# Where the modulation dots and the projection pieces stand among the steps of a head pair, in the first attention of a two-layer diffusion trunk

## The chip, the cores and the metric

One core of a Trainium2 chip runs the whole program: TensorE (PE, with its weight loads PEld), VectorE (DVE), ScalarE (ACT), GpSimd (POOL) and SyncE (SP), which issues all the DMAs. The metric is device time of one execution in microseconds; before the change the median of 3 runs is 1429.26 us (1427.46 to 1429.32).

## What is computed

Two layers over 1024 latent tokens and 256 context tokens of width 1024 (16 heads of 64). Each layer modulates its input, projects it, mixes, gates, projects out and normalises. Cut to what matters here:

```python
for i in range(DEPTH):                                            # DEPTH = 2
    shift, scale, gate = split(silu(c) @ w_ada[i] + b_ada[i], 3)  # the modulation; also with c_ctx
    u = h * (1 + scale) + shift
    y, yc = mixer_a(u, uc, ...) if i == 0 else mixer_b(u, uc, ...)
    h = layer_norm(ALPHA * h + gate * y, ...)

def mixer_a(u, uc, ...):
    q, k, v, g = split(u @ w_in)               # 16 query heads, 4 key/value heads
    q, k = rope(q), rope(k)                    # latents only
    # 128 queries at a time, against 3 blocks of 128 keys, the 256 context keys and a sink logit
    p = softmax(concat([mask(q @ k.T * scale), q @ k_ctx.T * scale, sink]))
    y = (p @ v * silu(g)) @ w_out
```

## The kernel before, in words

**Precision.** Every fp32 operand is split into a high and a low part, and a product is three matmuls (hi·hi, hi·lo, lo·hi), so TensorE is the busy engine throughout.

**The first attention (mixer a)** goes over 8 head pairs p. A pair has 20 *subs*: ten blocks b of 128 queries (8 of latents, 2 of context) for two heads h. Sub k = 20p + 2b + h does the following. `qkA` (L729): four score matmuls S_A (L739, L740) into a PSUM tile; `sm_first` (L308): DVE reads S_A, adds the mask and takes the row extreme (L320, I call it the *read* of S), POOL copies the sink in (L325), ACT takes the exponential (L327); `sm_second`: DVE reciprocal (L331), POOL scales (L332); `trA` (L753): TensorE transposes the 2, 4 or 5 blocks into another PSUM tile T_A (L339), ACT copies it out as the high part (L343), DVE subtracts for the low part (L345, the *split* of T); `pvA_fn` (L760): TensorE multiplies with the values (L768), and after each second block ACT and DVE combine the halves (L777, L779) and POOL gates (L782).

S_A and T_A share one PSUM tag `big` with **two** buffers (L97). So a T can begin only when the tile that had its buffer before has been let go: an S by its read L320, a T by its split L345; the same holds for an S.

**Steps.** `att_steps` (L786) makes the rows of this work. In the row where sub k's scores are issued, sub k-3 is transposed (AHEAD_A = 3) and one half of a block's value product is done. So in rows 0 to 2 of a pair the *last* three subs of the pair before are transposed, which are context blocks and narrow (two blocks, 256 columns), and the first scores of the new pair are issued. I call this place the *seam*. The rows of pair p are `rowsA[20p : 20p+20]`.

**Projection pieces.** Between the steps stand pieces of the projections for the gate of pair p and the queries of pair p+1: `gprojA(p) + qprojA(p+1)`, 48 pieces of three matmuls pj (L210 to L212), each 512 columns wide, or 256 for the context chunk. `merge` (L287) walks both lists by their costs: a piece is taken whenever the share of piece cost done is not above the share of step cost done. A step costs 545 for the transposes, 545 for the scores, 545 for half a value product; a piece 653 or 326. Evacuating a query chunk is the rope on DVE, POOL and ACT (L499 to L502) and the high and low parts for two heads (L694 on ACT, L695 on DVE, tiles qA).

**Modulation dots.** 48 dots (`dot_half`, L636) build the rest of the first layer's modulation and the second layer's in pairs 0 to 6 (SEG: 7 per pair, 6 in the last), off TensorE. One dot issues a DMA of 256 KB (L650, tile gw, two buffers), a multiply-and-sum on DVE (L652), a multiply on POOL (L653), and, at the next dot's place, a sum on ACT (L634). After the last of them `dots_end` (L658) does twelve small DVE operations (L662 to L667). Before the change they are inserted into the list of a pair's steps at positions 3, 12, 21 and so on, which is in rows 1, 3, 6, 9, 11, 14 and 17 or near them.

**What decides the order.** The program order of `merge` is not yet the order on the engines: the tile framework schedules each instruction by priority and by its own estimates, and `lift` (L130) raises some (the reads by LIFT_A = 80, the splits by 60). Each engine then takes its own list strictly in order. PSUM buffers of a tag are handed out in this scheduling as well, so which tile a T waits for can differ from row to row. Keys: the two heads' pairs 2q and 2q+1 share keys; `k_load(p // 2, 1)` (L713, tile kA) loads the second key tile of the new group when an even pair begins.

Of the kernel before, what the change touches and what calls it, by code (L numbers as in the profile page):

```python
# [38 lines left out]
GATED_LAST = 1 << 20  # L39

SEG = (7, 7, 7, 7, 7, 7, 6, 0)


def f32(ap):
    return ap.bitcast(F32)
# [37 lines left out]
def build(tc, i, out):  # L83
# [203 lines left out]
    def merge(att, fill, lead=0.0):  # L287

        ta = sum(a[0] for a in att) or 1.0
        tf = sum(f[0] for f in fill)  # L290
        ia = jf = 0
        ca = cf = 0.0
        while ia < len(att) or jf < len(fill):
            need = att[ia][2] if ia < len(att) and len(att[ia]) > 2 else 0
            if jf < len(fill) and (ia == len(att) or jf < need or cf - lead <= ca * (tf - lead) / ta):
                cf += fill[jf][0]
                fill[jf][1]()
                jf += 1
            else:
                ca += att[ia][0]  # L300
                att[ia][1]()
                ia += 1
# [333 lines left out]
    def dot_half(h, j):  # L636
        def run():
            dot_sum()
            if j == 0:
                gh.clear()  # L640
                for v in range(2):
                    t = px.tile([P, 512], F32, tag=f"gh{v}", bufs=1, name="gh")
                    dma(t, bass.AP(i["cr"].tensor, v * D + h * 512, [[0, P], [1, 512]]))
                    th = px.tile([P, 512], F32, tag="gw", bufs=2, name="gth")
                    nc.scalar.activation(th, t, AF.Tanh, scale=0.5)
                    nc.vector.scalar_tensor_tensor(t, th, 1.0, t, ALU.add, ALU.mult)
                    gh.append(t)
            acc = dhalf if h else dcol
            t = px.tile([P, 512], F32, tag="gw", bufs=2, name="gw")
            dma(t, i["wadaT"][j, :, h * 512 : (h + 1) * 512])  # L650
            o = ap_.tile([P, 512], F32, tag="ra", bufs=1, name="gj")
            nc.vector.tensor_tensor_reduce(o, t, gh[0], 0.5, 0.0, ALU.mult, ALU.add, accum_out=acc[:, j, 0:1])  # L652
            nc.gpsimd.tensor_tensor(t, t, gh[1], ALU.mult)  # L653
            sums.append((t, acc[:, j, 1:2]))

        return (0.0, run, 0)
# [12 lines left out]
    dots = [dot_half(h, j) for h in range(2) for j in range(24)]  # L669
# [29 lines left out]
    def qprojA(p):  # L699
        return proj_pieces(pos["Aq", p], uA, CHUNKS, rope_evac(q_store(p), ap_, 1))  # L700
# [9 lines left out]
    def k_load(kv, l):  # L710
        k = pq.tile([P, T], F32R, tag="kA", bufs=3, name=f"kA{kv}_{l}")
        for x in range(2):
            dma(f32(k[x * 64 : x * 64 + 64]), kdA[l, kv * 64 : kv * 64 + 64, :])  # L713
        kA[kv, l] = k

    def v_loadA(kv):
        v = pq.tile([P, 10, P], F32R, tag="vA", bufs=2, name=f"vA{kv}")
        dma(f32(v), vdA[:, kv, :].rearrange("(t p) e -> p t e", p=P))
        vA[kv] = v
# [40 lines left out]
    def pvA_fn(p, b, part):  # L760
        if b % 2 == 0 and part == 0:
            pvA[p] = psone(f"pvA{p}_{b}")
        o = pvA[p][:, (b % 2) * 256 : (b % 2) * 256 + 256]
        tl = tilesA(b)
        pt = ptA[p, b]
        for k, t in enumerate(tl):
            x = (pt.lo if part else pt.hi)[:, k].rearrange("p h q -> p (h q)")
            mm(o, vA[p // 2][:, t, :], x, start=k == 0 and not part, stop=part == 1 and k == len(tl) - 1)  # L768
        if not part:
            return  # L770
        del ptA[p, b]
        if b % 2 == 1:
            tmp = px.tile([P, 2, P], F32, tag="otmp", bufs=1, name="otmp")
            pv = pvA[p].rearrange("p (b h q) -> p b h q", b=2, h=2)
            heads = [(h, slice(h * 64, h * 64 + 64)) for h in range(2)]
            for h, hs in heads:
                nc.scalar.copy(tmp[hs], pv[64:128, :, h, :])  # L777
            for h, hs in heads:
                nc.vector.tensor_tensor(tmp[hs], pv[0:64, :, h, :], tmp[hs], ALU.add)  # L779
            tok = slice((b - 1) * P, (b + 1) * P)  # L780
            g = gA[p][:, tok]
            nc.gpsimd.tensor_tensor(g, tmp.rearrange("p b q -> p (b q)"), g, ALU.mult)  # L782
            if p == 7:
                dma(ogd[p][:, tok], g)
            elif b == 9:
                dma(ogd[p], gA[p])  # L786

    def att_steps(subs, qk, st, tr, pv, last_of_unit, costs, need, ahead, rise, split=False):

        seq = []  # L790
        n = len(subs)
        for k in range(-ahead, n + 2 + split):
            row = []

            def t_piece(k=k):
                if k + 1 < n:
                    with lift(rise(k)):
                        sm_second(st[k + 1])
                if k >= 0:
                    tr(k)  # L800

            def s_piece(k=k):
                qk(k + ahead)

            def v_piece(k=k):
                pv(k - 2)

            def v_first(k=k):
                pv(k - 2, 0)

            def v_second(k=k):
                pv(k - 3, 1)

            if -1 <= k < n:
                row.append((costs[0] if k >= 0 else 0.0, t_piece, 0))
            if k + ahead < n:
                row.append((costs[1], s_piece, 0))
            if split and 0 <= k - 2 < n and last_of_unit(k - 2):
                row.append((costs[2] / 2, v_first, 0))
            elif split and k - 3 >= 0 and last_of_unit(k - 3):  # L820
                row.append((costs[2] / 2, v_second, need(k - 3, k + ahead)))
            elif not split and k - 2 >= 0 and last_of_unit(k - 2):
                row.append((costs[2], v_piece, need(k - 2, k + ahead)))
            seq.append(row)
        return seq
# [3 lines left out]
    def needA(k, kq):  # L829
# [7 lines left out]
    rowsA = att_steps(  # L837
        subsA, qkA, stA, trA, lambda k, x: pvA_fn(*subsA[k][:2], x), lambda k: subsA[k][2] == 1,
        (545, 545, 1090), needA, AHEAD_A, lambda k: LIFT_A, True,
    )  # L840
# [3 lines left out]
    merge([], qprojA(0))  # L844
    px, px_st = pool("attA2", "right")
    for p in range(8):
        att = [x for row in rowsA[p * 20 : (p + 1) * 20] for x in row]
        if p % 2 == 0 and p:
            k_load(p // 2, 1)
        if p % 2 == 1 and p < 7:  # L850
            att.insert(20, (0.0, lambda p=p: k_load(p // 2 + 1, 0), 0))
            att.insert(24, (0.0, lambda p=p: v_loadA(p // 2 + 1), 0))
        if p < 7:
            n = len(att)
            for g in range(SEG[p]):
                att.insert(3 + g * (n // SEG[p] + 1), dots.pop(0))
            if not dots:
                att.append((0.0, dots_end, 0))
            merge(att, gprojA(p) + qprojA(p + 1), lead=0.0)
        else:  # L860

            att += [x for row in rowsA[8 * 20 :] for x in row]
            g7, fill = gprojA(7), []
            woA = OutWeights(up, "woA")
            for n, piece in enumerate(g7):
                fill.append(piece)
                if n >= 8:
                    fill.append((200.0, lambda j=n - 8: wo_piece(woA, i["wAo"], j)))
            assert len(fill) == G7_AT[2]
            oA0, yA0, zA0 = [], [], []  # L870

            def og_first():
                oA0.extend(og_small(og_load(0)))
                yA0.extend(psone(f"yA0_{nh}") for nh in range(2))

                for sl, x in zip(HALVES, ("whi", "wlo")):
                    zA0.append(f32(wp.tile([P, 512], F32R, tag=x, bufs=4, name="zA0")))
                    dma(zA0[-1], i["htok"][0][:, sl])

            fill.append((0.0, og_first))  # L880
            for n in range(2 * KT):
                fill.append((300.0, lambda n=n: out_part(yA0, HALVES[n // KT], oA0, woA, (n % KT,))))
            merge(att[:-6], fill, lead=1500.0)
            gts = up.tile([P, 2, D], F32, tag="l2", bufs=1, name="gates")
            for v in range(2):
                gate_rows(gts[:, v], dcol[:, 0:8, v])
            raw = og_load(1)
            merge(att[-6:], [])
# [42 lines left out]
    for b in range(10):  # L931
# [15 lines left out]
        g = gts[:, b // 8]  # L947
# [282 lines left out]
    for n, row in enumerate(rowsB):  # L1230
        ex = []
        if n < len(subsB):
            h, jp, r = subsB[n]
# [43 lines left out]
    att = [need7(x) for x in attB[last:]]  # L1277
# [35 lines left out]
    for b in range(8):  # L1313
        x = ob.tile([P, D], F32, tag="x", bufs=3, name="x")
# [127 lines left out]
```

## Time and profile before

| what | value |
|---|---|
| median of 3 runs (lowest, highest) | 1429.26 us (1427.46, 1429.32) |
| the profiled execution | 1428.33 us |
| its span, first to last instruction | 1426.5 us |
| mean granted TensorE clock | 0.997 |
| first attention: the windows 97 to 575 us | 478 us, of which PE busy 463.5, DVE 394.3, ACT 339.7, POOL 317.5 |

One pair takes about 60 us; the seams 0/1 to 6/7 lie at about 158, 218, 279, 340, 400, 460 and 521 us. How to read the rows of the profile: a line of the timeline gives start, duration, engine, line of the kernel, operation, tiles (written<-read) and form; in brackets stands the idle time of the engine just before, with what is thought to have ended it. A releaser is inferred; where several semaphores were awaited, the one named can be another that came late as well. Ends of matmuls are modelled; starts are measured.

### The profile page before, as it was taken

The page shows a single profiled execution, that of the slowest core. Times are in us where ns is not written, and L with a number is a line of the kernel's source. Part 1 is how long each engine was busy: PE and PEld are TensorE (multiplying, and loading weights), DVE is VectorE, ACT ScalarE, POOL GpSimd, SP SyncE. Part 2 cuts the span into 40 slices and gives each one's busy share as a digit, 9 for nine tenths or more (in the row PEclk, how much of TensorE's full clock was granted, in tenths as well). Part 3 has the DMA queues.
Part 4 walks back from the last instruction along what each step waited for, and adds up shares of the span by engine and source line. Part 5 has one row for each costly group of instructions (what it writes and reads, how often), then busy time and mean ns, then how long its engine had stood idle before and what let it go on. Part 6 is the DMA issues. An engine that isn't in the chain of part 4 may idle for free. (4 is left out here: it accounts for less than half of the span.)

```text
span 1426.5 us, 25166 instructions
## 1 busy us (share of the span) xinstructions
PE 1387.3 (97%) x8816; PEld 1214.8 (85%) x8816; DVE 971.8 (68%) x2203; ACT 731.3 (51%) x1559; POOL 643.6 (45%) x790
## 2 busy tenths in 40 slices
PE   8999999999999999999999999999999999998996
PEld 5888898888888888888898899888988899887785
DVE  4658887878878789566433765565665565667498
ACT  4337776677776778432222555554455454558200
POOL 0326766667666567233311333333233233338683
PEclk9999999999999999999999999999999999999998
DMA  9472114123222114344287575565655564485653
GB/s 367 174 239 79 52 64 125 53 79 97 74 72 63 57 65 143 127 133 133 71 257 219 159 210 167 138 188 149 176 148 169 145 195 142 118 222 169 179 149 108
DMA packets 127597, 202.39 MB, mean 142 GB/s; under 512 B 9712, under 2 KB 65392, under 8 KB 127472
## 3 DMA queue, kind: packets, MB, share of 16 engines
q1 hardware_dynamic: 127472, 200.79, 46.8%
q8 instruction: 70, 1.15, 0.3%
q14 instruction: 55, 0.45, 0.1%
HBM read 145.18 MB, written 55.57 MB: 141 GB/s over the span
## 5 line engine op out<-in xcount | busy, mean ns | idle before, releaser
L332 POOL TENSOR_SCALAR s_B<-s_B,rs_B 128x640 f32<-128x640 f32 (+1 forms) x128 | 101.9, 796 | 280.3 <-DVE rs_B L331 259.3
L210 PE MATMUL pj<-uBh,wh 128*128 128x512 f32 (+1 forms) x448 | 175.8, 392 | 0.0
L211 PE MATMUL pj<-uBl,wh 128*128 128x512 f32 (+1 forms) x448 | 170.2, 380 | 0.0
L212 PE MATMUL pj<-uBh,wl 128*128 128x512 f32 (+1 forms) x448 | 170.0, 379 | 0.0
L327 ACT ACTIVATE s_B<-s_B,m_B 128x640 f32<-128x640 f32 (+1 forms) x128 | 102.9, 804 | 124.0 <-DVE m_B L320 123.1
L327 ACT ACTIVATE s_A<-s_A,m_A 128x641 f32<-128x641 f32 (+2 forms) x160 | 119.5, 747 | 82.8 <-DVE m_A L320 59.6
L166 POOL TENSOR_TENSOR wl<-wr,wh 128x512 fp32r<-128x512 f32 x64 | 87.4, 1366 | 162.2 <-ACT wh L164 150.5
L332 POOL TENSOR_SCALAR s_A<-s_A,rs_A 128x640 f32<-128x640 f32 (+2 forms) x160 | 129.4, 809 | 64.7 <-DVE rs_A L331 58.7
L320 DVE CUSTOM_DVE_ANT_0 s_A<-S_A,msk,nsk 128x640 f32<-128x640 f32 (+2 forms) x160 | 123.6, 774 | 32.2 <-PE S_A L740 17.7
L345 DVE TENSOR_TENSOR pt_B<-T_B,pt_B 128x640 fp32r<-128x640 f32 (+1 forms) x128 | 100.8, 788 | 65.0 <-ACT pt_B L343 64.6
L210 PE MATMUL pj<-uAh,wh 128*128 128x512 f32 (+1 forms) x384 | 140.1, 365 | 0.8 <-DVE otmp L779 0.8
L211 PE MATMUL pj<-uAl,wh 128*128 128x512 f32 (+1 forms) x384 | 137.7, 359 | 0.0
L212 PE MATMUL pj<-uAh,wl 128*128 128x512 f32 (+1 forms) x384 | 137.2, 357 | 0.0
L345 DVE TENSOR_TENSOR ptl_A<-T_A,pth_A 128x640 fp32r<-128x640 f32 (+2 forms) x160 | 114.1, 713 | 17.4 <-PE pvA L768 10.4
L339 PE MATMUL T_A<-ident,s_A 128*128 128x128 f32 x672 | 100.9, 275 | 10.0 <-DVE m_A L320 4.5
L343 ACT CAST pt_B<-T_B 128x640 fp32r<-128x640 f32 (+1 forms) x128 | 84.4, 660 | 50.0 <-PE T_B L339 49.2
L339 PEld LDWEIGHTS T_A<-ident,s_A 128*128 128x128 f32 x672 | 77.4, 140 | 36.6 <-issue 9.8
L320 DVE CUSTOM_DVE_ANT_0 s_B<-S_B,bias 128x640 f32<-128x640 f32 (+1 forms) x128 | 100.3, 784 | 8.7 <-PE S_B L1077 8.1
L343 ACT CAST pth_A<-T_A 128x640 fp32r<-128x640 f32 (+2 forms) x160 | 96.4, 602 | 17.2 <-PE T_A L339 15.7
L212 PEld LDWEIGHTS pj<-uBh,wl 128*128 128x128 f32 x448 | 84.3, 188 | 16.7
L339 PE MATMUL T_B<-ident,s_B 128*128 128x128 f32 x608 | 88.2, 274 | 8.1 <-DVE pt_B L345 3.2
L339 PEld LDWEIGHTS T_B<-ident,s_B 128*128 128x128 f32 x608 | 70.2, 140 | 26.7 <-issue 10.9
(222 smaller groups left out, 3893.7 us busy)
## 6 DMA issues: line engine op xcount, KB each, us to landing
kB<-kdB SPq DMA_DIRECT2D x64, 320.0 KB, 5.4
gw<-in_wadaT SPq DMA_DIRECT2D x48, 256.0 KB, 2.8
vdB<-st SPq DMA_DIRECT2D x20, 512.0 KB, 3.5
vB<-vdB SPq DMA_DIRECT2D x16, 640.0 KB, 4.7
wada<-in_wadaC SPq DMA_DIRECT2D x16, 512.0 KB, 9.6
kdB<-st SPq DMA_DIRECT2D x16, 512.0 KB, 2.8
qdB<-st SPq DMA_DIRECT2D x16, 512.0 KB, 3.6
qB<-qdB SPq DMA_DIRECT2D x32, 256.0 KB, 4.6
```

What stands on the lines that cost most here:

```text
L166: e.tensor_tensor(lo, r, f32(hi), ALU.subtract)
L210: mm(pt[:, :n], hi[:, sl], rh, start=kt == 0, stop=False)
L211: mm(pt[:, :n], hi[:, sl], rl, start=False, stop=False)
L212: mm(pt[:, :n], lo[:, sl], rh, start=False, stop=kt == KT - 1)
L320: nc.vector.tensor_tensor_reduce(outp, sc, in1, scale, init if init is not None else 3e38, ALU.add, ALU.min, accum_out=s.m)
L327: nc.scalar.activation(s.t[:, :n], s.t[:, :n], AF.Exp, bias=s.m, scale=-1.0, accum_out=s.sum)
L332: nc.gpsimd.tensor_scalar(s.t[:, : s.w], s.t[:, : s.w], s.rs, 1.0, ALU.mult, ALU.mult)
L339: nc.tensor.transpose(tp[:, k * P : (k + 1) * P], s.t[:, src * P : (src + 1) * P], ident)
L343: nc.scalar.copy(pt.hi[:, :n, hl, :], tv)
L345: nc.vector.tensor_tensor(pt.lo[:, :n, hl, :], tv, f32(pt.hi[:, :n, hl, :]), ALU.subtract)
```

## The change

Two things for pairs 0 to 6, both in the rows' order. The steps of the first six rows of a pair get their cost times 1.25 in `merge`, so that more projection pieces fall between them, and fewer between the later ones. The dots are taken out of the even spacing and stand behind rows 6, 8, 10, 12, 14, 16 and 18. The two loads for the next keys and values are attached to rows 7 and 9 of odd pairs instead of positions 20 and 24. Pair 7 keeps its order of steps. No instruction is added or removed.

```diff
+SEAM, SEAM_FILL = 6, 1.25
...
-        att = [x for row in rowsA[p * 20 : (p + 1) * 20] for x in row]
+        att = []
...
+        for r, row in enumerate(rowsA[p * 20 : (p + 1) * 20]):
+
+            seam = p < 7 and r < SEAM
+            att += [(x[0] * SEAM_FILL if seam else x[0], *x[1:]) for x in row]
...
+            if p < 7 and r >= SEAM and r % 2 == 0 and (r - SEAM) // 2 < SEG[p]:
+                att.append(dots.pop(0))
         if p < 7:
-            n = len(att)
-            for g in range(SEG[p]):
-                att.insert(3 + g * (n // SEG[p] + 1), dots.pop(0))
```

What this does on the engines, at three places. Numbers behind S_A, T_A, s_A are the sub; line numbers of the changed kernel are higher by 2.

VectorE at the seam from pair 3 to pair 4, before: the split of T_A77 stands behind a dot (gj, L652) and one of the context parts of the query.

```order
L320 ISA s_A79_4294,m_A79_4295<-S_A79_4291,msk_141,nsk_142 128x256
L320 ISA m_A79_4295 128x1
L695 TENSOR_TENSOR qA8_4060<-ra_4217,qA8_4060 64x512
L345 TENSOR_TENSOR ptl_A76_4282<-T_A76_4283,pth_A76_4281 128x2x128
L695 TENSOR_TENSOR qA9_4061<-ra_4217,qA9_4061 64x512
L331 RECIPROCAL rs_A79_4297<-sum_A79_4296 128x1
L695 TENSOR_TENSOR qA8_4060<-pj24_2_4238,qA8_4060 64x256
L652 ISA gj_4367,dhalf_733<-gw_4365,gh_3815 128x512
L652 ISA dhalf_733 128x1
L345 TENSOR_TENSOR ptl_A76_4282<-T_A77_4337,pth_A76_4281 128x2x128
L695 TENSOR_TENSOR qA9_4061<-pj24_2_4238,qA9_4061 64x256
L345 TENSOR_TENSOR ptl_A78_4373<-T_A78_4374,pth_A78_4372 128x2x128
```

The same place after the change:

```order
L322 ISA s_A79_4294,m_A79_4295<-S_A79_4291,msk_141,nsk_142 128x256
L322 ISA m_A79_4295 128x1
L781 TENSOR_TENSOR otmp_4226<-pvA3_4_4103,otmp_4226 64x256
L347 TENSOR_TENSOR ptl_A76_4282<-T_A76_4283,pth_A76_4281 128x2x128
L697 TENSOR_TENSOR qA8_4042<-ra_4201,qA8_4042 64x512
L697 TENSOR_TENSOR qA9_4043<-ra_4201,qA9_4043 64x512
L333 RECIPROCAL rs_A79_4297<-sum_A79_4296 128x1
L347 TENSOR_TENSOR ptl_A76_4282<-T_A77_4337,pth_A76_4281 128x2x128
L654 ISA gj_4276,dhalf_733<-gw_4274,gh_4006 128x512
L654 ISA dhalf_733 128x1
L697 TENSOR_TENSOR qA8_4042<-pj24_2_4232,qA8_4042 64x256
L697 TENSOR_TENSOR qA9_4043<-pj24_2_4232,qA9_4043 64x256
```

The dot is still near the seam (it is the one of row 18 of pair 3), but the split of T_A77 now stands ahead of it.

TensorE in row 4 of pair 5, between the scores S_A103 and the transposes T_A101, which take over the buffer of S_A103; pj are the projection's matmuls, pvA the value product. Before, four pj and two pvA stand between:

```order
L740 MATMUL S_A103_5254<-kA2_1_4316,qA11_4872 128x256
L210 MATMUL pj30_0_5139<-uAh0_105,wh31_4718 128x512
L211 MATMUL pj30_0_5139<-uAl0_108,wh31_4718 128x512
L212 MATMUL pj30_0_5139<-uAh0_105,wl31_4719 128x512
L768 MATMUL pvA4_8_5237<-ptl_A96_5093,vA2_3791 128x256 x2
L210 MATMUL pj30_1_5290<-uAh1_106,wh30_4714 128x512
L339 MATMUL T_A101_5283<-ident_63,s_A101_5192 128x128 x4
```

After the change three pj stand between S_A103 and the pvA, as before, and from there on:

```order
L770 MATMUL pvA4_8_5234<-ptl_A96_5093,vA2_3898 128x256 x2
L212 MATMUL pj30_1_5267<-uAh1_106,wh30_4679 128x512
L213 MATMUL pj30_1_5267<-uAl1_109,wh30_4679 128x512
L214 MATMUL pj30_1_5267<-uAh1_106,wl30_4680 128x512
L341 MATMUL T_A101_5278<-ident_63,s_A101_5189 128x128 x4
```

Two more pj stand between the scores and the transposes that wait for their buffer.

TensorE in row 10 of pair 4, between S_A89 and T_A87, which takes over the buffer of S_A89. Before, three narrow pj stand between S_A89 and this pvA, and then:

```order
L768 MATMUL pvA4_0_4576<-ptl_A82_4506,vA2_3791 128x256 x5
L210 MATMUL pj26_2_4618<-uAh2_107,wh27_3907 128x256
L211 MATMUL pj26_2_4618<-uAl2_110,wh27_3907 128x256
L212 MATMUL pj26_2_4618<-uAh2_107,wl27_3908 128x256
L210 MATMUL pj28_0_4726<-uAh0_105,wh28_4319 128x512
L211 MATMUL pj28_0_4726<-uAl0_108,wh28_4319 128x512
L212 MATMUL pj28_0_4726<-uAh0_105,wl28_4320 128x512
L339 MATMUL T_A87_4732<-ident_63,s_A87_4601 128x128 x5
```

After the change the pvA follows S_A89 at once:

```order
L742 MATMUL S_A89_4695<-kA2_1_4316,qA9_4043 128x256
L770 MATMUL pvA4_0_4567<-ptl_A82_4500,vA2_3898 128x256 x5
L212 MATMUL pj28_0_4691<-uAh0_105,wh28_4319 128x512
L213 MATMUL pj28_0_4691<-uAl0_108,wh28_4319 128x512
L214 MATMUL pj28_0_4691<-uAh0_105,wl28_4320 128x512
L341 MATMUL T_A87_4723<-ident_63,s_A87_4599 128x128 x5
```

Six narrow pj have gone from between the two.

More of the change, by code (lines that the diff above doesn't have):

```diff
@@ L846, in build @@
     for p in range(8):
-        att = [x for row in rowsA[p * 20 : (p + 1) * 20] for x in row]
+        att = []
         if p % 2 == 0 and p:
             k_load(p // 2, 1)
-        if p % 2 == 1 and p < 7:
-            att.insert(20, (0.0, lambda p=p: k_load(p // 2 + 1, 0), 0))
-            att.insert(24, (0.0, lambda p=p: v_loadA(p // 2 + 1), 0))
+        for r, row in enumerate(rowsA[p * 20 : (p + 1) * 20]):
+            seam = p < 7 and r < SEAM
+            att += [(x[0] * SEAM_FILL if seam else x[0], *x[1:]) for x in row]
+            if p % 2 == 1 and p < 7 and r in (7, 9):
+                att.append((0.0, lambda p=p, f=k_load if r == 7 else v_loadA: f(*((p // 2 + 1, 0)[: 2 if f is k_load else 1])), 0))
+            if p < 7 and r >= SEAM and r % 2 == 0 and (r - SEAM) // 2 < SEG[p]:
+                att.append(dots.pop(0))
         if p < 7:
-            n = len(att)
-            for g in range(SEG[p]):
-                att.insert(3 + g * (n // SEG[p] + 1), dots.pop(0))
             if not dots:
```

## The prediction

> **What bounds the kernel now.** I began with the page: which engine fills the span.
>
> ```profile
> span 1426.5 us, 25166 instructions
> PE 1387.3 (97%) x8816; PEld 1214.8 (85%) x8816; DVE 971.8 (68%) x2203; ACT 731.3 (51%) x1559; POOL 643.6 (45%) x790
> ```
>
> TensorE is busy for 97%, so a change that adds and removes no instruction can win only what PE idles, and lose only by new idling. The view of waits, for PE, says what the first attention's idling waits for (us, times, longest).
>
> ```profile
> PE T_A L339 <- DVE m_A L320: 4.5, 6, 1.2
> PE T_A L339 <- POOL s_A L332: 3.5, 5, 0.9
> ...
> PE S_A L740 <- DVE ptl_A L345: 2.0, 7, 0.7
> PE S_A L739 <- DVE ptl_A L345: 1.6, 2, 1.1
> ```
>
> Together 11.6 us in 20 waits of a transpose or a score tile, all for a buffer that VectorE frees. Where they lie, the windows tell: seam 3/4, then most of the rest of pair 4 (stretch, length, then busy us of PE, PEld, DVE, ACT, POOL).
>
> ```profile
> 334.00:349.00 15.00, 14.05 (x83) 11.27 (x82) 11.80 (x30) 9.53 (x25) 10.40 (x15) 1.00 0.55 140
> 349.00:394.00 45.00, 44.66 (x302) 40.12 (x302) 37.37 (x92) 32.39 (x72) 30.58 (x43) 1.00 0.24 77
> ```
>
> PE idles .95 us in the 15 us of the seam and .34 in the 45 us behind it, at a granted clock of 1.00. DVE is about as busy in one (79%) as in the other (83%), so the seam suffers from order rather than from load. The timeline of that seam:
>
> ```profile
> 338.19 1.03 DVE L652 CUSTOM_DVE_ANT_0 gj<-gw,gh 128x512 f32<-128x512 f32 x1
> 338.39 0.40 PE L212 MATMUL pj<-uAh,wl 128*128 128x512 f32 x1
> 339.15 0.41 DVE L345 TENSOR_TENSOR ptl_A<-T_A,pth_A 128x256 fp32r<-128x256 f32 x1
> 339.70 0.41 PE L339 MATMUL T_A<-ident,s_A 128*128 128x128 f32 x2 [0.92 <-POOL s_A L332]
> 341.87 0.51 PE L739 MATMUL S_A<-kA,qA 128*128 128x256 f32 x2
> ```
>
> T_A78 at 339.70 takes the buffer of T_A77, whose split ran only at 339.15, right behind the dot of 1.03. The page names POOL as the releaser, but what ended last before the transposes is the split (339.56). The five other seams, with the dot at 277.45 standing in the same way ahead of a read:
>
> ```profile
> 218.37 0.30 PE L339 MATMUL T_A<-ident,s_A 128*128 128x128 f32 x1 [0.93 <-POOL s_A L332]
> 277.45 1.03 DVE L652 CUSTOM_DVE_ANT_0 gj<-gw,gh 128x512 f32<-128x512 f32 x1
> 277.90 0.40 PE L212 MATMUL pj<-uAh,wl 128*128 128x512 f32 x1
> 278.41 0.74 DVE L320 CUSTOM_DVE_ANT_0 s_A<-S_A,msk,nsk 128x512 f32<-128x512 f32 x1
> 279.31 0.41 PE L339 MATMUL T_A<-ident,s_A 128*128 128x128 f32 x2 [1.01 <-DVE m_A L320]
> 400.30 0.30 PE L339 MATMUL T_A<-ident,s_A 128*128 128x128 f32 x1 [1.02 <-DVE m_A L320]
> 459.68 0.30 PE L339 MATMUL T_A<-ident,s_A 128*128 128x128 f32 x1 [0.93 <-POOL s_A L332]
> 520.99 0.30 PE L339 MATMUL T_A<-ident,s_A 128*128 128x128 f32 x1 [1.24 <-DVE m_A L320]
> ```
>
> The brackets add up to .93 + 1.01 + .92 + 1.02 + .93 + 1.24 = 6.05 us. They are too small. In row 4 of pair 4:
>
> ```profile
> 347.57 0.28 PE L740 MATMUL S_A<-kA,qA 128*128 128x256 f32 x1
> 348.00 0.88 DVE L320 CUSTOM_DVE_ANT_0 s_A<-S_A,msk,nsk 128x640 f32<-128x640 f32 x1
> 348.39 0.39 PE L211 MATMUL pj<-uAl,wh 128*128 128x512 f32 x1
> 348.61 0.39 PE L212 MATMUL pj<-uAh,wl 128*128 128x512 f32 x1
> 349.04 0.63 PE L339 MATMUL T_A<-ident,s_A 128*128 128x128 f32 x4
> 349.42 0.68 DVE L652 CUSTOM_DVE_ANT_0 gj<-gw,gh 128x512 f32<-128x512 f32 x1
> ```
>
> A wide pj takes .22 us from start to start (348.39 to 348.61), though its row says .39. So the transposes at 339.70 could have begun at 338.39 + .22 = 338.61: 1.09 us were lost where the bracket has .92. At 279.31 it is 1.19 for 1.01. I add .17 to each of six: 7.0 us. The Trainium skill ("Perfetto Trace Analysis", section "Tensor Engine Instruction (MATMUL, LD_WEIGHTS)") says that the profiler computes a matmul's end and doesn't observe it; by the reported ends the loss would be 6.05 and the sum below 1.0 smaller; the starts here speak for 7.0.
>
> The same rows show a smaller loss without a bracket: T_A81 could begin at 348.61 + .22 = 348.83 and began at 349.04, .2 late. From the last score matmul (347.57) to the transposes that want its buffer, DVE's .43 to start, .88 to read and .16 to the first transpose make 1.47 us, and the two pieces between don't fill that.
>
> **The change part by part.**
>
> *Dots away from the seams.* By the new order the split or read that frees the buffer stands ahead of the dot at all six seams; 7.0 us is to be had. What is late next:
>
> At the three seams into even pairs (218, 340, 460), the second half of the scores S_A80 needs the key tile kA that is loaded there (the queue's rows; then POOL's subtraction that frees the buffer of the load ahead of it; then the tile's line).
>
> ```profile
> 335.27 0.33 SPq L150 DMA_DIRECT2D wr<-in_wAg  x1
> 335.69 1.09 SPq L713 DMA_DIRECT2D kA<-kdA  x2
> 333.95 1.29 POOL L166 TENSOR_TENSOR wl<-wr,wh 128x512 fp32r<-128x512 f32 x1 [0.77 <-PE T_A L339]
> DMA to landing us min/median/max: 4.1/5.2/8.3
> ```
>
> The second of the two issues is at about 336.2; with 5.2 us it lands at 341.4, and PE came there at 341.87, so today the stall covers it. Without the stall, and with one pj instead of three ahead of it, PE comes at 338.61 + about .2 (two transposes) + .67 (three pj) + .45 (four pvA, half as wide as a pj) + .22 = 340.2. The load itself also moves: L166 waited .77 for transposes that now have more work spread around them; I give it .6 of that, so landing 340.8. That would be a wait of .6; with the minimum landing it is none, with the load unmoved 1.2. I take .5: three times, 1.5.
>
> At the two odd seams (279, 400) the read can start where the dot did, at 277.45, end .74 later, and let the transposes in .15 later, at 278.34, against a PE free at 278.12: .2 each, .4. At seam 6/7 DVE has other work ahead of the read:
>
> ```profile
> 516.77 0.67 DVE L652 CUSTOM_DVE_ANT_0 gj<-gw,gh 128x512 f32<-128x512 f32 x1
> 518.27 0.83 DVE L662 TENSOR_TENSOR dcol<-dcol,dhalf 128x24 f32<-128x24 f32 x1
> 520.08 0.75 DVE L320 CUSTOM_DVE_ANT_0 s_A<-S_A,msk,nsk 128x512 f32<-128x512 f32 x1
> ```
>
> The read must come 1.24 + .17 = 1.41 earlier; .67 of dot and about 1.0 of the small operations move ahead of it: I keep .1. The transposes after the stall, no longer preceded by rest, may wait .1 at the three even seams: .3. Left over: 1.5 + .4 + .1 + .3 = 2.3, so the seams give 7.0 − 2.3 = 4.7 us (3.0 to 7.0).
>
> *More pieces in rows 0 to 5.* The share of the pieces there goes from .300 to 1.25 × .300 / (1 + .25 × .300) = .349 of 48: about 2.3 narrow-and-wide pieces, in the order some two wide ones (six pj, 1.3 us) per pair. They lie in rows 3 to 5, ahead of transposes such as T_A81 and T_A101 (the order above has two pj more there, .44 us, which covers the .2). Such .2 stand at some nine places (the transposes of row 4 of all six pairs 1 to 6, of row 3 of the even ones): 9 × .2 = 1.8 gained.
>
> *What the later rows pay.* Those pieces are missing in rows 6 to 19. By the new order four transposes a pair (rows 10, 13, 14, 16; T_A87 is shown above) have three pj less, .66 us, between them and the scores or transposes whose buffer they take: about 1.41 us from start to start where 1.47 is needed. Those rows waited little before, and mostly at one place in each pair:
>
> ```profile
> 386.88 0.38 PE L740 MATMUL S_A<-kA,qA 128*128 128x256 f32 x1 [0.21 <-DVE ptl_A L345]
> 242.30 0.41 PE L339 MATMUL T_A<-ident,s_A 128*128 128x128 f32 x2 [0.47 <-DVE m_A L320]
> 300.28 0.45 PE L739 MATMUL S_A<-kA,qA 128*128 128x384 f32 x1 [0.53 <-DVE ptl_A L345]
> ```
>
> The score tile at 386.88 (.21 + .17 = .38) comes back in six pairs; the others are single. Walking rows 4 to 16 of pair 4 through in the new order with the durations of the rows above, I find seven waits of .04 to .21, together .80, where there were about .6 (the .38 and one of .2): .2 per pair, 1.2 for six. The lower bound is a gain of 2.3 (the six .38 go, nothing new), the upper is under the rivals.
>
> *The dots in their new place.* Each dot's DVE and POOL time is as before, from this group (minimum, median, maximum ns):
>
> ```profile
> L652 DVE CUSTOM_DVE_ANT_0 gj<-gw,gh x48: 670/692/1822, 113.7 to 516.8; 128x512 f32<-128x512 f32 x48
> L653 POOL TENSOR_TENSOR gw<-gw,gh x48: 1277/1292/1305, 114.5 to 517.8; 128x512 f32<-128x512 f32 x48
> DMA to landing us min/median/max: 2.6/2.8/4.3
> ```
>
> Dots now follow each other every two rows, about 6 us (339.70 − 279.31 is 60.4 for 20 rows). The load (2.8, at most 4.3, two buffers) is covered by that; its issue on SP now stands among the weight loads of rows 6 to 18 and no longer near kA. POOL's 1.29 lies beside other work, but ACT's sum waits for it and holds the copies of T (L343) behind itself, which a split waits for: that is in the .21 of my walk. If two of these met at a row, the cost is up to 1.3 there. A dot takes .68 at 349.42 and 1.03 at 338.19 and 277.45; in the middle rows I take .68, and 1.03 as the upper end. The Trainium skill ("SBUF — State Buffer", section "Who interferes with whom") has a DVE instruction with two SBUF inputs contend with a GpSimd instruction that reads SBUF; by that a dot issued behind POOL's 1.29 could lose all of it, which would put .6 more on a read that it delays; the maximum of 1.82 allows it, and the median of .69 says that it is rare. The moved loads (rows 7 and 9 of odd pairs) are issued on SP many rows ahead of their use: nothing. First pair: ramp-up rules it, nothing, give or take 1.5. Pair 7 keeps its order: nothing.
>
> *Sum.* 4.7 + 1.8 − 1.2 = 5.3 us. The profiled execution is 1428.33 us (span 1426.5 and 1.8 around it), .9 below the median: 1423.0 by it, and 1424.0 by the median of 1429.26.
>
> **The rivals.**
>
> *Everything goes.* The kA loads land in time, the reads come early enough, and with fewer pieces the score tiles of row 16 no longer wait: 7.0 + 1.8 + 6 × .38 = 11.1 us, 1418.2. For it: DVE has 17% of rest in the middle rows. Against it: kA's 5.2 us, and narrower gaps make waits of this kind more often than they end them. Chance .11.
>
> *The gain is eaten at the same seams.* kA lands where it did (3 × 1.2), the odd reads keep .4, .4 more remain, and the middle rows cost 1.2 + 2.1: 7.0 + 1.8 − 3.6 − .8 − 3.3 = 1.1 us gained, 1428.2, within a measurement's reach. For it: issue and landing of kA are shown, my .6 earlier is only argued. Against it: POOL's rest of .77 is real. Chance .22.
>
> *Slower: dots ahead of the reads in the middle rows.* Each pair now has four transposes with .66 less cover in rows that hold all the dots; a dot ahead of the read that frees the buffer delays it by .68 to 1.03, as at the seams today. That is the present stall, moved from 6 places to 24. The seams and row 4 give 6.5; from a mean of 6.5 / 24 = .27 us per transpose the kernel is slower. At .5 it is 12 − 6.5 = 5.5 us slower, 1434.8; at the whole .66 it is 9.3, 1438.6. For it: the seam rows show the price of exactly this; DVE is at 83% there. Against it: in the walk the read mostly comes first, and only two of seven waits in pair 4 pass .15. Chance .12.
>
> That the change doesn't do what it says is ruled out by the order: dots and pieces do move.
>
> **How the numbers follow.** Forecast .55, all goes .11, eaten .22, slower .12. 1424.0 is the forecast's; its own bounds (seams 3.0 to 7.0, row 4 1.0 to 1.8, later rows −2.5 to 0, first pair 1.5 either way) run to 1420 and 1428. The range goes 1419.0 to 1430.5: past the top of the eaten case with the scatter of runs (1427.46 to 1429.32), leaving out most of the two outer cases. .2% is 2.86 us, about what a measurement of this kernel can tell from no change: faster .55 + .11 = .66, same .22, slower .12.
>
> **What would show it.** Right: idle before the transposes at the six seams under .3; PE's window of the seam at 15 us with .3 to .6 idle, in even pairs ended by a DMA of kA; T_A81 within .05 of the pj before; small waits of .1 to .2 in rows 10 to 16. Wrong: brackets of .5 and more at T_A87, T_A88 and their like in other pairs behind a DVE dot (the slower case); waits over 1 us for kA (the eaten one); seams still idle behind another DVE operation; or a mean of L652 well over .8 us.

## The result and the profile after

| | before | after |
|---|---|---|
| median (lowest, highest) | 1429.29 (1427.46, 1431.63), 6 runs | 1434.77 (1432.27, 1436.22), 6 runs |
| ratio | | 1.0034, 95% interval 1.0024 to 1.0044 |
| profiled execution, span | 1428.33, 1426.5 | 1434.77, 1433.0 |

The change made the kernel 5.5 us slower, where 5.3 us of gain were forecast. Where the first attention ends, by the timelines of both kernels (the first matmul behind it):

```profile
577.95 0.43 PE L375 MATMUL gate<-ident,dcol 128*128 128x128 f32 x2
```

```profile
582.78 0.43 PE L377 MATMUL gate<-ident,dcol 128*128 128x128 f32 x2
```

4.8 us were lost by there. The spans differ by 6.5. The other 1.7 come in the second attention, which the change doesn't touch; the medians differ by 5.5, so I put most of the 1.7 down to these two executions, which no run shows. The view of waits for PE, after:

```profile
PE T_A L341 <- DVE m_A L322: 5.9, 10, 1.9
...
PE S_A L741 <- DVE ptl_A L347: 3.6, 5, 0.9
PE T_A L341 <- DVE ptl_A L347: 2.9, 7, 0.6
```

Before, 11.6 us in 20 waits; now these three rows alone have 12.4 in 22, and they name DVE only. The windows, with pair 4 some 1.5 us later than before:

```profile
335.00:350.00 15.00, 13.93 (x81) 11.47 (x82) 12.03 (x32) 10.03 (x27) 10.95 (x16) 1.00 0.51 140
350.00:395.00 45.00, 44.33 (x299) 39.76 (x298) 36.81 (x90) 31.94 (x72) 30.55 (x41) 1.00 0.23 77
```

PE idles 1.07 us at the seam (.95 before) and .67 behind it (.34): the seam kept its loss and the middle doubled. A wait of .76 for the score tile of the last row of pair 3 ended at 335.00, so it lies just ahead of the first window. The timeline of the last rows of pair 1 shows how a seam looks now (POOL, DVE and PE in order of time):

```profile
211.53 1.30 POOL L168 TENSOR_TENSOR wl<-wr,wh 128x512 fp32r<-128x512 f32 x1
211.64 1.73 DVE L504 TENSOR_TENSOR ra<-ra,rb 128x512 f32<-128x512 f32 x1
...
214.23 0.48 DVE L322 CUSTOM_DVE_ANT_0 s_A<-S_A,msk,nsk 128x256 f32<-128x256 f32 x1
214.87 0.41 PE L341 MATMUL T_A<-ident,s_A 128*128 128x128 f32 x2 [0.59 <-DVE m_A L322]
215.59 0.42 DVE L347 TENSOR_TENSOR ptl_A<-T_A,pth_A 128x256 fp32r<-128x256 f32 x1
216.07 0.39 PE L741 MATMUL S_A<-kA,qA 128*128 128x256 f32 x1 [0.79 <-DVE ptl_A L347]
```

The stall of 1.09 at 218.37 is gone. In its place T_A37 waits .59 for the read at 214.23 and S_A40 waits .79 for the split at 215.59; by the starts .75 and .95, together 1.70. No dot stands on VectorE in these rows. The read is late because the sum of the rope (L504) took 1.73 us, from .11 after POOL's subtraction for a weight began to .54 after it ended. The groups of that line, before and after:

```profile
L502 DVE TENSOR_TENSOR ra<-ra,rb 128x512 f32<-128x512 f32 x14 | 10.0, 711 | 0.1
```

```profile
L504 DVE TENSOR_TENSOR ra<-ra,rb 128x512 f32<-128x512 f32 x14 | 13.1, 933 | 1.4 <-POOL rb L503 1.4
```

3.1 us more over 14, and three of them, in pairs 1, 4 and 5, took 1.72 to 1.74 where most take .69. By the starts those three seams lose 1.70 each. This is the rule that the prediction quoted from the Trainium skill ("SBUF — State Buffer", section "Who interferes with whom") for the dots: two SBUF inputs on VectorE, a GpSimd instruction that reads SBUF, and the later one waits for the end of the first. The trace agrees within .15 us: the sum ended .54 after POOL's operation did, where it takes .68 alone. The instruction that it hit was not the dot. In the changed kernel without the dots (below) the same two meet in the other order: the sum begins at 207.62 and takes .68, POOL's subtraction begins .11 later and takes 1.73 instead of 1.30.

For all seams and rows I set each T_A's and S_A's first start against the matmul before it plus that matmul's spacing, and count what is over .1 us, for pairs 1 to 6. The seam's row has the T_A of the last three subs and the S_A of the last two and of the first; the first S_A of pair 1 (1.2 before, 1.0 after, .6 without dots) is in it, though seam 0/1 is none of the six. The second half of a pair's first score tile, which needs the key tile kA, has a row of its own. Four runs of the experiments below stand beside it.

| us of PE waiting for a buffer, pairs 1 to 6 | before | after | before, no dots | after, no dots | fill alone | dots alone |
|---|---|---|---|---|---|---|
| T_A of rows 3, 4, 5 | 2.1 | 0 | 1.4 | 0 | .5 | 2.5 |
| T_A of row 6 | 1.1 | 1.1 | 1.1 | 1.1 | 1.2 | 1.2 |
| middle rows | 4.4 | 10.5 | 3.5 | 1.5 | 7.1 | 8.7 |
| seam | 8.7 | 9.5 | .9 | 2.3 | 6.7 | 11.2 |
| waiting for kA | 0 | .5 | 3.9 | 2.1 | 1.9 | 0 |
| sum, from unrounded values | 16.3 | 21.7 | 10.9 | 7.0 | 17.4 | 23.5 |

### The profile page after: what moved, and what is told of

It is laid out like the page before. It is cut to its first block, busy times and chain, and to the rows that moved or that the text cites. A ratio compares the mean times of both kernels' runs of the same rounds, so it can differ in the third digit from the quotient of the medians.

```text
span 1433.0 us, 25144 instructions
## 1 busy us (share of the span) xinstructions
PE 1390.4 (97%) x8816; PEld 1216.2 (85%) x8816; DVE 975.1 (68%) x2203; ACT 729.3 (51%) x1559; POOL 646.6 (45%) x790
## 5 line engine op out<-in xcount | busy, mean ns | idle before, releaser
L212 PE MATMUL pj<-uAh,wh 128*128 128x512 f32 (+1 forms) x384 | 144.7, 377 | 0.0
L341 PEld LDWEIGHTS T_A<-ident,s_A 128*128 128x128 f32 x672 | 74.4, 140 | 37.8 <-POOL s_A L334 11.1
```

The lines of the kernel that those rows point to most:

```text
L212: mm(pt[:, :n], hi[:, sl], rh, start=kt == 0, stop=False)
L341: nc.tensor.transpose(tp[:, k * P : (k + 1) * P], s.t[:, src * P : (src + 1) * P], ident)
```

## The experiments

The theories, by the letters of the expectations: D, the dots' places cost the time; F, the missing pieces do; P, the dot alone makes the seam stall; V, VectorE's list is late; L, VectorE stands still behind POOL (below this is the lock), against O, the order alone; G, VectorE waits for the dots' loads. Where an expectation speaks of the transposes "of row 8", it means sub 8 of the pair, which is transposed three rows later; the text here says row 11, and so with the transposes of the other rows. All times are medians with the ratio to the kernel before in the same comparison (its median there was 1429.5 to 1430.3).

### One half of the change at a time

Dots alone:

```diff
-SEAM, SEAM_FILL = 6, 1.25
+SEAM, SEAM_FILL = 6, 1.0
```

> The change's dots (rows 6 to 18) and loads, but the pieces spread evenly as before (factor 1.0). Theory D (the dots in every second row of the later part cost the time: they stand ahead of reads and splits of S and T there, and move POOL's subtractions onto the rope): 1432 to 1436 us, with waits of .6 at the transposes of row 8 and the waits at the last three rows of a pair still there. Theory F (the fill costs the time: later rows have too few pieces to cover the waits): 1423 to 1427 us, seams free, no waits in rows 8 to 16.

1435.58, ratio 1.0043 (1.0031 to 1.0055). Fill alone (the insertions of before put back, the factor 1.25 kept):

> The dots and loads where they stood before, and the first six rows' costs times 1.25. Theory D: 1427 to 1430 us, the seam stalls of 1.1 us as before, the .2 in rows 3 and 4 gone. Theory F: 1433 to 1437 us, with new waits in rows 7 to 15 although no dot was moved.

1433.55, ratio 1.0021 (1.0012 to 1.0030). Neither theory stands: each half alone loses, 6.1 and 4.1 by the medians (the fill's ratio makes it 3.0), and both together no more than one. The table says why they don't add up: the dots alone bring the seam to 11.2, the fill alone takes the small waits away and puts others into the middle, three of which are 1.1 to 1.7 at row 10.

Two other placings:

```diff
-if p < 7 and r >= SEAM and r % 2 == 0 and (r - SEAM) // 2 < SEG[p]:
+if p < 7 and r >= 4 and r % 2 == 0 and (r - 4) // 2 < SEG[p]:
```

> As the change, but the dots stand behind rows 4 to 16 instead of 6 to 18. Theory D with the dot of row 18 and of row 16 near the seam as the cause of the new waits in the last rows of a pair: 1429 to 1432 us. Theory D with the dots' density as the cause wherever they begin: 1433 to 1436 us. Theory F: 1433 to 1436 us.

1434.22, ratio 1.0034 (1.0021 to 1.0047): two rows earlier is no better.

```diff
-att.insert(3 + g * (n // SEG[p] + 1), dots.pop(0))
+att.insert(3 + g * 8, dots.pop(0))
```

(in the kernel before)

> The kernel before, with the dots a little closer (positions 3, 11, 19 to 51 instead of 3, 12, 21 to 57), so that the last one of a pair stands some two rows ahead of the seam; no other edit. If the dot alone makes the seam stall: 1422 to 1426 us. If something else of VectorE's is late at the seam as soon as the dot is gone (the rope of the query's last chunk): 1428 to 1431 us, with waits of .7 to 1 us a row earlier.

1444.11, ratio 1.0103 (1.0088 to 1.0117): far outside both ranges, from moving dots by a row or two. It doesn't test whether the dot alone makes the seam stall: the dot there is the first one of the next pair, at position 3, which the edit leaves in place, and five of the six stalls stayed, 1.08 to 1.18 by the starts. Its timeline shows a price that the prediction had at nothing, the dot's load:

```profile
315.26 0.33 SPq L150 DMA_DIRECT2D wr<-in_wAq  x1
...
315.68 0.38 SPq L650 DMA_DIRECT2D gw<-in_wadaT  x1
...
320.36 0.69 DVE L652 CUSTOM_DVE_ANT_0 gj<-gw,gh 128x512 f32<-128x512 f32 x1 [2.75 <-DMA gw<-in_wadaT]
320.98 0.88 DVE L320 CUSTOM_DVE_ANT_0 s_A<-S_A,msk,nsk 128x640 f32<-128x640 f32 x1
322.01 0.30 PE L339 MATMUL T_A<-ident,s_A 128*128 128x128 f32 x1 [3.10 <-DVE m_A L320]
```

The load is issued on SP behind a weight's, lands 4.7 us later, the dot waits 2.75 for it with VectorE standing still, the read waits behind the dot, and PE 3.10 behind the read. VectorE's waits for gw in all: 11.5 us here, 9.8 with the fill alone, 7.7 with the dots alone, but .9 before and .5 after. So this path costs something in the halves, and next to nothing in the whole change. In the fill alone the three waits at row 10 stand behind such dots (1.7 to 2.0 us of VectorE's waiting each). In the dots alone the seams' largest waits, 1.40 in four pairs, have another cause: the query's two low parts (L697) stand ahead of the split there and take 1.2 and 1.1 us, where .69 is usual, beside POOL's subtraction and its gating, and no load is late. The load's path was tried on the fill alone:

```diff
+if j == 0: gw_load(h, 0)
+t = gwt.pop((h, j))
+if j < 23: gw_load(h, j + 1)
-t = px.tile([P, 512], F32, tag="gw", bufs=2, name="gw")
-dma(t, i["wadaT"][j, :, h * 512 : (h + 1) * 512])
```

> The fill alone (dots where they stood before), with each dot's load issued one dot earlier, into the buffer that the dot before has just given back; the orders of TensorE, VectorE and ScalarE are those of the fill alone, word for word. In the fill alone VectorE stood 9.8 us waiting for these loads. Theory G (this waiting cost what the fill alone lost): VectorE's wait for gw falls below 2 us, the three waits of 1.1 to 1.7 at the transposes of row 7 go, 1427 to 1430 us. If VectorE's waiting was covered: 1432 to 1434 us as the fill alone.

1433.44, ratio 1.0025 (1.0017 to 1.0034), and VectorE's wait is 10.4 us. That tells nothing of G: the load that the dot at 186 us needs was issued at 183.01, in the fill alone at 182.84, because on SP it stayed behind the same weight load. The edit asked for an earlier load and got none. Another run of the fill alone gave 1431.09:

> A placeholder that repeats the fill alone once: 1430 to 1435 us.

### POOL's subtraction in four pieces

```diff
-e.tensor_tensor(lo, r, f32(hi), ALU.subtract)
+w = 128 if 8 <= j < NA else 512
+for x in range(0, 512, w):
+    e.tensor_tensor(lo[:, x : x + w], r[:, x : x + w], f32(hi[:, x : x + w]), ALU.subtract)
```

> The kernel before with the same edit. Theory L: the dot at the seams goes from 1.03 to about .8 and the query's low part from 1.1 to .8, the six stalls shrink from 1.1 to .6 or so, 1425 to 1428 us. Theory O: stalls as before, 1429 to 1431 us.

> The changed kernel, with POOL's subtraction for the low part of a weight done in four pieces of 128 columns instead of one of 512; TensorE's, VectorE's and ScalarE's orders differ in some twenty rows. Theory L (the new waits in the last rows of a pair come from VectorE operations with two SBUF inputs, the rope's sum and the query's low part, that stand still until POOL's 1.3 us subtraction is over): the sum L504 goes from 1.73 to about 1.0 or less where it was stretched, the waits of .75 and .95 there shrink by half or more, 1429 to 1432 us. Theory O (it is the order of VectorE's list, whatever POOL does): same waits, 1434 to 1436 us, or a little more, for POOL has more instructions.

Before with it: 1428.42, ratio .9990 (.9981 to .9999), a time between the two theories' ranges. Five of the six seam stalls shrink as theory L has it, by the starts from 1.1 or 1.2 to .6 or .7 (the sixth stays at 1.40), and the middle rows wait 1.1 longer. In pair 1 the bracket goes from .93 to .47:

```profile
216.57 1.73 POOL L168 TENSOR_TENSOR wl<-wr,wh 128x128 fp32r<-128x128 f32 x3
216.69 0.89 DVE L654 CUSTOM_DVE_ANT_0 gj<-gw,gh 128x512 f32<-128x512 f32 x1
217.51 0.41 DVE L347 TENSOR_TENSOR ptl_A<-T_A,pth_A 128x256 fp32r<-128x256 f32 x1
218.07 0.30 PE L341 MATMUL T_A<-ident,s_A 128*128 128x128 f32 x1 [0.47 <-DVE ptl_A L347]
```

After with it: 1446.50, ratio 1.0115 (1.0101 to 1.0129), 12 us worse than the change. At the seam theory L holds again, by the timeline of the same place:

```profile
212.71 1.74 POOL L170 TENSOR_TENSOR wl<-wr,wh 128x128 fp32r<-128x128 f32 x3 [0.17 <-ACT wh L166]
212.82 0.90 DVE L506 TENSOR_TENSOR ra<-ra,rb 128x512 f32<-128x512 f32 x1
...
215.30 0.38 PE L343 MATMUL T_A<-ident,s_A 128*128 128x128 f32 x2
...
216.40 0.39 PE L743 MATMUL S_A<-kA,qA 128*128 128x256 f32 x1 [0.72 <-DVE ptl_A L349]
```

The rope's sum takes .90 for 1.73, the transposes don't wait, the score tile still does (.72). What it cost is elsewhere: four pieces take POOL about 2.2 us instead of 1.3, the weights' loads that wait for them hold up the dots' loads on SP, and VectorE waited 10.2 us for gw where it had waited .5. The worst place (POOL's pieces ended at 434.4, the weight's load was issued at 434.43 and the dot's behind it at 434.86):

```profile
440.03 0.69 DVE L656 CUSTOM_DVE_ANT_0 gj<-gw,gh 128x512 f32<-128x512 f32 x1 [3.42 <-DMA gw<-in_wadaT]
440.65 0.82 DVE L349 TENSOR_TENSOR ptl_A<-T_A,pth_A 128x640 fp32r<-128x640 f32 x1
441.61 0.45 PE L343 MATMUL T_A<-ident,s_A 128*128 128x128 f32 x1 [3.23 <-DVE ptl_A L349]
```

So the lock is shown, and the whole loss is not laid to it by this.

### No dots, half dots

```diff
 def run():
+    if j == 0:
+        nc.vector.memset(dhalf if h else dcol[:, 0:24], 0.0)
+    return
```

> The kernel before without the 48 dots: their loads, VectorE's, POOL's and ScalarE's parts are left out, the sums are zeros; the rest stands nearly as before. Theory P (the prediction's: the dot alone makes the seam stall, and what is late next is small): the six stalls of 1.1 go to .3 or less, 1421 to 1424 us. Theory V (VectorE's list of the last rows of a pair is late by itself, the rope of the query's last chunk ahead of the splits, and the dot only adds to it): waits of .5 or more stay at the seams, at the transposes or at the score tile a row earlier, 1424 to 1428 us.

> The changed kernel without the dots, so the fill alone. Theory P: faster than the same without the fill by the .2 of rows 3 and 4, 1419 to 1423 us. Theory V: the score tile at the end of each pair still waits .5 to .9, the transposes of row 13 .25, and it ends at 1424 to 1428 us, no faster than the kernel before without dots. Theory F (the pieces taken from the later rows cost the time): 1429 to 1433 us, slower than the kernel before without dots by what the change lost.

1422.33, ratio .9945 (.9931 to .9959), and 1417.77, ratio .9916 (.9903 to .9930). These are the runs that settle most. In the kernel before, the six stalls of 1.1 and more fall to .13 or less when the dots go, so theory P holds for it. Without dots the fill, with the moved loads, is worth 4.6 us. That this is near the 5.3 forecast for the whole change is chance: the prediction's terms for the pieces alone make 1.8 − 1.2 = .6, theory P's range for this run began at 1419, and of the difference 1.8 us are a shorter wait for kA. With the dots the change loses 5.5. So the 48 dots cost 7.9 us before and 17.0 after, and 17.0 − 7.9 − 4.6 = 4.5 are the change's loss, up to the 1.0 by which the kernel before's median differs between the two comparisons. One wait appeared where the prediction had expected one, the key tile of an even pair:

```profile
219.82 0.36 PE L742 MATMUL S_A<-kA,qA 128*128 128x256 f32 x1 [2.15 <-DMA kA<-kdA]
```

In the three even pairs it comes to 3.9 us by the starts here, and to 2.1 in the changed kernel without dots.

Then one part of each dot, in the changed kernel (without the two lines of POOL's part, or without VectorE's):

> The changed kernel with only the load and VectorE's part of each dot; POOL's multiply and ScalarE's sum are left out. Theory V (VectorE's own time, .69 each and in every second row, makes the reads late): keeps most of the 17 us that the dots cost, 1428 to 1433 us. Theory L (POOL's multiply holds up VectorE, and pushes POOL's weight subtractions onto the rope): keeps a third or less, 1419 to 1424 us.

> The changed kernel with only the load, POOL's multiply and ScalarE's sum of each dot; VectorE's part is left out. Theory V: 1419 to 1424 us. Theory L: 1427 to 1432 us, with VectorE's rope sums still stretched from .69 towards 1.7. If the two parts only cost together, both kernels are near 1420.

1432.14, ratio 1.0015 (1.0006 to 1.0024), and 1427.71, ratio .9985 (.9976 to .9994). Over the 1417.8 without dots, VectorE's part alone costs 14.4 us and POOL's with ScalarE's 9.9, 17.0 together. The first is theory V's number and the second theory L's: with POOL's part alone the rope's sum still took over 1.0 us in seven of 14. The trace of VectorE's part alone says how:

```profile
182.30 1.29 POOL L168 TENSOR_TENSOR wl<-wr,wh 128x512 fp32r<-128x512 f32 x1
182.33 1.81 DVE L655 CUSTOM_DVE_ANT_0 gj<-gw,gh 128x512 f32<-128x512 f32 x1
184.07 0.87 DVE L322 CUSTOM_DVE_ANT_0 s_A<-S_A,msk,nsk 128x640 f32<-128x640 f32 x1
185.10 0.30 PE L341 MATMUL T_A<-ident,s_A 128*128 128x128 f32 x1 [1.50 <-DVE m_A L322]
```

A dot of .69 takes 1.81 because POOL's weight subtraction began .03 earlier, and 1.1 of the 1.5 us that PE waits is that; a dot of 1.81 stands there in all six pairs (PE loses 1.66 to 1.68 by the starts). V and L were not rivals: the dot's place in VectorE's list and POOL's subtraction beside it make the price together.

### Other rows, as dense

Same edit as for rows 4 to 16, with other first rows.

> The change with the dots in rows 0, 2 to 12 of a pair, as dense as in rows 6 to 18. If the place at the end of the pair costs the time: the waits of the last four rows (9.0 us in pairs 1 to 6) fall to 3 or less, 1426 to 1429 us. If the spacing costs it, wherever the dots begin: 1432 to 1436 us.

> The change with the dots in rows 1, 3 to 13, where the other half of a value product is done. Place: 1425 to 1429 us as in rows 0 to 12. Spacing: 1432 to 1436 us. If what matters is beside which half of the value product a dot falls (the waits of .6 in row 8 stand behind dots in even rows): faster than rows 0 to 12 by 3 us or more.

1438.81, ratio 1.0060 (1.0046 to 1.0074), and 1430.04, ratio 1.0006 (.9997 to 1.0015). One row's shift is worth 8.8 us, so neither place at the end of a pair nor spacing is the cause by itself. Odd rows looked like it:

> The change with the dots in odd rows 5 to 17, between the rows 4 to 16 (1434.2 us) and 6 to 18 (1434.8 us) that were run. If odd rows are what helps: 1427 to 1431 us, without the waits of .6 in row 8. If the place does (early rows good, late rows bad): 1433 to 1436 us.

> The change with the dots in odd rows 7 to 19, one row later than in the change. If odd rows help: 1428 to 1432 us, the seams a little worse than in rows 5 to 17. If the place does: 1434 to 1438 us.

1442.48, ratio 1.0083 (1.0070 to 1.0097), and 1454.07, ratio 1.0162 (1.0149 to 1.0176). That theory fell at once. The timeline of rows 5 to 17 shows a third path from a dot to PE, without a load, and through ScalarE's list:

```profile
206.82 0.75 DVE L654 CUSTOM_DVE_ANT_0 gj<-gw,gh 128x512 f32<-128x512 f32 x1
206.99 1.73 POOL L655 TENSOR_TENSOR gw<-gw,gh 128x512 f32<-128x512 f32 x1
208.67 0.18 POOL L327 COPY s_A<-nsk 128x1 f32<-128x1 f32 x1
208.75 0.63 ACT L636 ACTIVATE gw<-gw 128x512 f32<-128x512 f32 x1 [3.36 <-POOL gw L655]
...
209.38 0.50 ACT L329 ACTIVATE s_A<-s_A,m_A 128x257 f32<-128x257 f32 x1
210.00 0.16 DVE L333 RECIPROCAL rs_A<-sum_A 128x1 f32<-128x1 f32 x1 [2.43 <-ACT s_A L329]
210.71 0.47 DVE L322 CUSTOM_DVE_ANT_0 s_A<-S_A,msk,nsk 128x256 f32<-128x256 f32 x1
...
211.33 0.41 PE L341 MATMUL T_A<-ident,s_A 128*128 128x128 f32 x2 [1.90 <-DVE m_A L322]
```

POOL's multiply of a dot begins .17 after VectorE's part of the dot and takes 1.73 instead of 1.29. ScalarE's sum of that dot waits for it with ScalarE idle for 3.36 us, the exponential stands behind the sum in ScalarE's list (and the sink's copy, which it needs too, behind the multiply on POOL), the reciprocal waits for the exponential, and the next tile's read stands behind the reciprocal. So VectorE rests 2.43 us, though that read's scores were begun at 207.85. The same rest of 2.42 stands in each of pairs 1 to 6, and PE's waits there, 2.03 to 2.06 in five and 2.7 in the last, come to 12.9 us, where this kernel as a whole lost 12.3.

A mixture, pair 0 in rows 6 to 18 and the others in rows 1 to 13:

> The change with the dots of pair 0 in rows 6 to 18 as in the change and those of pairs 1 to 6 in rows 1 to 13. If the pairs add up (8.75 us of idling in pair 0 with rows 1 to 13, 5.79 with rows 6 to 18, the rest as in rows 1 to 13): 1426 to 1428.5 us, faster than the kernel before. If a pair's placing changes the next pair's: 1429 to 1433 us.

1428.57, ratio .9990 (.9981 to .9999), a little ahead of the kernel before (and level with its narrow subtraction), by about what a measurement can tell. I found none that is clearly ahead.

One more part of the change's loss, pair 6, where the twelve small operations behind the last dot stand. After, by the timeline:

```profile
512.00 1.73 POOL L655 TENSOR_TENSOR gw<-gw,gh 128x512 f32<-128x512 f32 x1
512.74 1.02 DVE L664 TENSOR_TENSOR dcol<-dcol,dhalf 128x24 f32<-128x24 f32 x1
...
513.81 1.32 POOL L655 TENSOR_TENSOR gw<-gw,gh 128x512 f32<-128x512 f32 x1
514.02 1.13 DVE L667 SCALAR_TENSOR_TENSOR colA<-dcol,lnc 128x8 f32<-128x8 f32 x1
...
515.78 0.46 DVE L322 CUSTOM_DVE_ANT_0 s_A<-S_A,msk,nsk 128x256 f32<-128x256 f32 x1
...
516.40 0.30 PE L341 MATMUL T_A<-ident,s_A 128*128 128x128 f32 x1 [1.94 <-DVE m_A L322]
```

Two tiny operations (24 and 8 columns) take 1.02 and 1.13 beside the multiplies of the last dots. Moving the closing part into pair 7:

```diff
-if not dots:
-    att.append((0.0, dots_end, 0))
 ...
+att.insert(15, (0.0, dots_end, 0))
```

> The changed kernel with the twelve small operations that close the dots moved from the end of pair 6 into the sixth row of pair 7. If they are the cause of the 2.1 us wait of pair 6's transposes in row 15 and of the .7 at the seam behind it: 1431.5 to 1433.5 us. If another operation is late there as soon as they are gone: 1434 to 1436 us.

1437.56, ratio 1.0057 (1.0042 to 1.0072). The wait at 516 stayed, 2.5 by the starts: the scheduler kept four of the operations in the same place, ahead of the read (1.02 and 1.33 us now), and pair 7 waited some 2 us longer than in the change (5.8 for 3.7 by the starts). So the edit tells nothing of what the place without them is worth.

## Why the prediction was wrong

**The step that failed** is *Dots away from the seams*: "By the new order the split or read that frees the buffer stands ahead of the dot at all six seams; 7.0 us is to be had", with 2.3 left over, so a gain of 4.7; measured was a loss of 1.5 at these six (from 7.5 to 9.0 with the wait for kA, without seam 0/1). The order is as it was said, and the six waits did go: 7.0 to 1.05 us in the T_A that had them. But the term asked what stands directly ahead of the split, not when VectorE gets there. In the new order POOL's subtraction fell on the rope's sum in three of the pairs, which made it 1.05 us longer (1.73 − .68), and a read that stands a row ahead of the old stall came late. In pair 1 it began at 214.23 (213.34 before), while PE could have begun the transposes at 214.12 (214.97 before). Without dots the changed kernel has 3.8 at these six seams, 2.1 of it for kA, against the 2.3 of the left-over: the working comes nearer for a kernel whose VectorE isn't late, but its 1.5 for kA was too small.

Behind it stands a price: *The dots in their new place* gave each dot its .68 to 1.03 and only where it stands directly ahead of a read. Left out, the dots show 17.0 us in the new rows for 7.9 in the old.

**The later rows** were put at 1.2; the middle went from 4.4 to 10.5, so 6.1 (2.1 of it in pair 6, for which the prediction had no term). The small waits of .25 in row 16's transposes (1.6 in six pairs) are the missing pieces, for they stay without dots (1.4). The rest, the .6 of row 11 in five pairs above all, goes with the dots. There the split waits for ScalarE's copy, which ends in the same tenth as the dot ahead of the split; which of them holds it isn't told apart. With either part of the dots left out row 11 has no wait in any of the six pairs, so neither part alone makes it.

**What was right.** Rows 3 and 4: 1.8 forecast, 2.1 gone. The row that waited .38 six times lost it too (2.3), which stood only in the rival where everything goes. The wait for kA was put at .5 three times; after shows one of .5, since PE is late for another reason. Without dots it is 1.2, .4 and .5 after, and 2.4, .9 and .6 before, by the starts: the wait was real, more than was put down for it, and mostly covered in the change. The fill by itself, with the moved loads, is a gain of 4.6 us without dots, where .6 was forecast for the pieces.

**The rivals.** The slower one gave 1434.8 for a mean of .5 us a transpose, and 1434.8 was measured. That is better than it deserves: "a dot ahead of the read that frees the buffer delays it by .68 to 1.03" is one of several paths that the runs show, and the price it worked from is that of VectorE alone. The path through ScalarE's sum was named in the prediction and taken as covered by the walk's .21; in rows 5 to 17 it cost 2.0 a pair. The rival's main point holds for the middle rows, where most of the new waits go when the dots go; but the seams, which it let win, lost as well. The chance of .12 came from "in the walk the read mostly comes first": a walk with median durations can't show an operation of .69 that takes 1.8. The rule quoted in the prediction from the Trainium skill spoke against the change, and was set aside with "the median of .69 says that it is rare". Rare is enough where each costs 1 us: 12 of the 48 dots took over .9 already in the kernel before.

**Open** is why this order puts POOL's subtraction on the rope's sum in pairs 1, 4 and 5: it follows from when POOL's list reaches it, and no run held that moment fixed. And .7 to .9 of the score tile's wait at the seam stays when the lock is weakened; without dots it is .17 or .18 in five pairs and .57 in pair 1 (1.45 in six).

## What to carry to other kernels

Ahead of an engine at 97%, an engine at 80% has no room in its list: ask of each moved operation not what stands beside it but what is behind it in strict order on every engine that it uses, here VectorE's list, POOL's list and the DMA queue. Price a filler operation by the worst duration that the trace shows for it, and look which engine's operation makes it so. To learn what filler costs, leave it out once: one such run of each kernel showed 7.9 us before and 17.0 after, and that the other half of the change was good.

## What was not expected of the hardware

The blocked time of a VectorE operation is in its duration, not in the idle column: L504 of .68 is shown as 1.73, L667 over 8 columns as 1.13 (.17 alone), a dot as 1.81. Subtracting 512 columns on POOL in one operation takes 1.3 us, in four of 128 about 2.2 (.55 each). Which of two such operations is stretched goes by which began first: the rope's sum in the change (1.73), POOL's subtraction in the same place without dots (1.73). Placing the same dots of .69 us in other rows moved the whole kernel between 1428.6 and 1454.1 us, without any change in the work of an engine.
